# A hybrid decoder step: two weight slices scaled by their largest values, the first cast on GpSimd, loaded ahead of the second token tile, and the bias-table matmuls at later places in the program

## The chip, the cores and the metric

One core of a Trainium2 chip runs the whole program. Its engines are TensorE (matmuls, PE in the profile, with weight loads listed as PEld), VectorE (DVE), ScalarE (ACT), GpSimd (POOL) and SyncE (SP), whose queue issues nearly all transfers. The metric is the device time of one execution in microseconds (us), the median of several runs.

## The reference

One layer and one inference step, for a prompt of 2048 rows of 1024 and 8 sample rows:

```
h = rmsnorm(x, norm_g)
z = h @ w_in          # one matrix, its columns split among three mixers and their gates
A: q 512 | k 128 | v 128 | gate 512      sliding window of 128, 8 heads, 2 kv heads,
                                         logits = q.k/8 + rel_bias, learned sink per head
B: u 512 | v 512 | gate 512              chunked gMLP: u * (W_s v + b), causal 128x128
C: q 256 | k 256 | v 512 | gate 512 | r 16   gated linear attention, chunks of 64
x = x + concat[A*silu(gA), B*silu(gB), C*silu(gC)] @ w_out
y = rmsnorm(x, final gain)
```

The bias of mixer A depends on the distance between query and key alone, so the program makes one table of it (128 x 8 x 256) and adds it to the scores of every token tile.

## The kernel before, in words

**Numbers.** Values in fp32 are held as two fp16 parts, a high one (a cast of the scaled value) and a low one (the remainder, scaled value minus high part). Each product is three matmul passes, high by high, high by low, low by high, accumulated in one PSUM bank.

**Tokens.** There are 16 tiles of 128 tokens, two to a chunk of 256. `h_tile` (called through `norm_split`) squares a loaded tile on ScalarE with a row sum (L244), works out the reciprocal root of the mean on VectorE in a chain of 128x1 instructions (L246, then L124 to L134), casts the high part on ScalarE (L248), makes the low part on VectorE (L249), and has each part transposed by a DMA on SP (L258), which fills `hT`, the left or right side of every projection matmul. Loads of tiles are issued on SP by `x_load` (L240).

**Weight slices.** `prep_slice` brings a group of columns of `w_in` onto the chip in four parts (L164). Here matter A1 (k, v and r: 272 columns), A0 (q: 512) and A2 (gate: 512). `sq` squares each quarter with a row sum on ScalarE (L179), `sq2` adds over partitions with a matmul by ones (L185), bounds the scale and rounds it to a power of two (L187 to L192), and `split` makes, for each of 8 blocks, the high part on ScalarE (L203) and the low part on VectorE (L204). The A1 and A0 stages live in buffers named `hb`, A1's result in `s`, A0's in `sl`; `gs` is the scale by row, `invs` its inverse.

**Units.** Matmuls come in units: `unit_va` (v and r of one tile, through `mm_tok`, L307), `unit_k` and `unit_q` (k, and a quarter of q, of one chunk, through `mm_col`, L296), `unit_gate` (L307, then tanh on ScalarE L486 and a product on VectorE L487). Each writes a bank `pp` of which there are four; scores, tables and small sums use four banks `mx`.

**Bias table.** `lc_bias` multiplies the bias values by a table of distances (L384), copies the result, writes it to DRAM (`e_d`) and reads it back so that each partition holds a shifted row (`Lp`). `lc_bm` mirrors that with four fp32 matmuls of 128x512 (L398), and VectorE scales each into `BM`, which the scores' eviction (L510) reads.

**Order.** The function is written as a straight program. Side work is put in by `at(t, f)`, where t is a count of matmul columns issued so far divided by 2400, and `tick` runs what is due:

```
at(1.0, lambda: h_tile(2))
at(2.0, lc_bias)
at(7.0, lc_bm(0))
at(9.0, lc_bm(1))
```

A scheduler then reorders the instructions into one queue for each engine, and each engine works through its own in order. An instruction wrapped in `tc.keep_in_program_order` keeps its place among its engine's instructions. Scores of tile n are due at 17 + 6.5 x (2n), tanh and evictions follow their matmuls. Before the first unit come, in this order: load of tile 0, small constants, load of tile 1, loads of A1, first part of A0, `h_tile(0)`, A1's `sq` and `sq2`, `h_tile(1)`, A1's two halves of `split`, and the rest.

Of the kernel before, what the change touches and what calls it, by code (L numbers as in the profile page):

```python
# [15 lines left out]
AF = mybir.ActivationFunctionType  # L16
ALU = mybir.AluOpType
AX = mybir.AxisListType
# [15 lines left out]
OFF = {}  # L34
# [9 lines left out]
def hybrid_step_kernel(ctx: ExitStack, tc: tile.TileContext, I, O):  # L44
    nc = tc.nc
    V, S, G, PE, SP = nc.vector, nc.scalar, nc.gpsimd, nc.tensor, nc.sync
# [20 lines left out]
    def nm(s):  # L67
        cnt[0] += 1
        return f"{s}_{cnt[0]}"

    def small(shape, dt=F32, tag=None):
        w = 1
        for d in shape[1:]:
            w *= d
        return sm.tile(shape, dt, tag=tag or f"sm{w}", name=nm("sm"), bufs=1 if tag in ONE else 2 if tag in TWO else 8 if w <= 16 else 4)
# [4 lines left out]
    def mbank():  # L80
        return psm.tile([128, 512], F32, tag="mx", name=nm("mx"))

    def hbuf(shape, dt):
        return hp_.tile(shape, dt, tag="hT", name=nm("hb"))

    def slot(shape, dt):
        return sl_.tile(shape, dt, tag="slot", name=nm("sl"))
# [30 lines left out]
    def chain(p, n):  # L118
        t = sm.tile([p, 8 * n], F32, tag=f"ch{n}", name=nm("ch"), bufs=CHB[n])
        return [t[:, i * n:(i + 1) * n] for i in range(8)]  # L120
# [16 lines left out]
    def pow2_scale(ch, base_inv, s_out, inv_out):  # L137
        T, e = ch[0].bitcast(I32), ch[1].bitcast(I32)
        V.tensor_scalar(out=e, in0=T, scalar1=24, scalar2=None, op0=ALU.logical_shift_right)
        si, ii = ch[2].bitcast(I32), ch[3].bitcast(I32)  # L140
        V.tensor_scalar(out=si, in0=e, scalar1=-1.0, scalar2=205.0, op0=ALU.mult, op1=ALU.add)
        V.tensor_scalar(out=ii, in0=e, scalar1=1.0, scalar2=float(base_inv), op0=ALU.mult, op1=ALU.add)
        V.tensor_scalar(out=s_out.bitcast(I32), in0=si, scalar1=23, scalar2=None, op0=ALU.logical_shift_left)
        V.tensor_scalar(out=inv_out.bitcast(I32), in0=ii, scalar1=23, scalar2=None, op0=ALU.logical_shift_left)  # L144
# [2 lines left out]
    LOADP = {}  # L147
    INVI = {}

    def prep_slice(name, idx, cols, stage, dst, nload=1):  # L150
        n = sum(w for _, w in cols)
        inv = invs[:, idx:idx + 1]
        INVI[name] = inv
        st = {}

        def load_part(a, b):
            if "sg" not in st:
                st["sg"] = stage()
            for ap, k0, k1 in st["sg"]:
                lo, hi = max(a, k0), min(b, k1)  # L160
                c = 0
                for off, w in cols:
                    if lo < hi:
                        SP.dma_start(out=ap[:, lo - k0:hi - k0, c:c + w],  # L164
                                     in_=w_in[lo * 128:hi * 128, off:off + w].rearrange("(k p) n -> p k n", p=128))
                    c += w

        def load():
            for a in range(0, 8, 2):
                load_part(a, a + 2)  # L170

        def sq():
            st["dst"] = dst()
            SL[name] = st["dst"]
            acc = small([128, 4])
            for ap, k0, k1 in st["sg"]:
                for k in range(k0, k1, 2):
                    jk = st["dst"][:, 0, k:k + 2, :].bitcast(BF16)
                    S.activation(out=jk, in_=ap[:, k - k0:k - k0 + 2], func=AF.Square, accum_out=acc[:, k // 2:k // 2 + 1])  # L179
            st["acc"] = acc  # L180

        def sq2():
            acc = st["acc"]
            ps = mbank()
            PE.matmul(ps[:, 0:4], ones, acc, start=True, stop=True)  # L185
            ch = chain(128, 1)
            V.tensor_reduce(out=ch[5], in_=ps[:, 0:4], axis=AX.X, op=ALU.add)  # L187
            V.tensor_scalar(out=ch[0], in0=ch[5], scalar1=gmax2, scalar2=2e-20, op0=ALU.mult, op1=ALU.max)
            s = ch[4]
            pow2_scale(ch, 39, s, inv)  # L190
            gs = sm.tile([128, 8], F32, tag="gs", name=nm("gs"), bufs=3)
            V.tensor_scalar(out=gs, in0=gcol, scalar1=s, scalar2=None, op0=ALU.mult)  # L192
            st["gs"] = gs

        def split(a, b):
            def f():
                for ap, k0, k1 in st["sg"]:
                    for k in range(max(a, k0), min(b, k1)):
                        src = ap[:, k - k0, :]
                        hi = st["dst"][:, 0, k, :]  # L200
                        lo = st["dst"][:, 1, k, :]
                        gk = st["gs"][:, k:k + 1]
                        S.activation(out=hi, in_=src, func=AF.Copy, scale=gk)  # L203
                        V.scalar_tensor_tensor(out=lo, in0=src, scalar=gk, in1=hi, op0=ALU.mult, op1=ALU.subtract)  # L204
            return f

        LOADP[name] = [(lambda a=a: load_part(a, a + 2)) for a in range(0, 8, 2)]
        return [load, sq, sq2, split(0, 4), split(4, 8)]

    def stage_h(n):  # L210
        def f():
            return [(hbuf([128, 4, n], F32), 0, 4), (hbuf([128, 4, n], F32), 4, 8)]
        return f
# [6 lines left out]
    def dst_slot(n):  # L220
        return lambda: slot([128, 2, 8, n], F16)

    def dst_one(n):
        return lambda: one.tile([128, 2, 8, n], F16, tag="s1", name=nm("s1"))
# [7 lines left out]
    def x_bufs(j):  # L232
        if not xst:
            xst[0], xst[1] = slot([128, 4096], F32), slot([128, 4096], F32)
        b = xst[j // 2][:, (j % 2) * 2048:(j % 2 + 1) * 2048]
        return b[:, 0:DM], b[:, DM:2 * DM].bitcast(F16).rearrange("p (a b) -> p a b", a=2)

    def x_load(t):
        xt, _ = x_bufs(t % 4)
        SP.dma_start(out=xt, in_=xp[t * 128:(t + 1) * 128, :])  # L240
# [10 lines left out]
    def h_tile(t):  # L251
        c, j = divmod(t, 2)
        if j == 0:
            h_alloc(c)
        xt, xh = x_bufs(t % 4)
        norm_split(xt, xh, 128)
        for hl in range(2):
            SP.dma_start_transpose(out=hT[c][:, hl, :, j * 128:(j + 1) * 128], in_=xh[:, hl, :])  # L258
# [17 lines left out]
    def at(t, *fs):  # L276
        for f in fs:
            cnt[0] += 1
            bisect.insort(EV, (t, cnt[0], f))
# [71 lines left out]
    def startup_consts():  # L351
        G.memset(ones, 1.0)
        make_identity(nc, ident)
        SP.dma_start(out=gcol, in_=I["norm_g"][0].rearrange("(k p) -> p k", p=128))
        gm = small([128, 1])
        V.tensor_reduce(out=gm, in_=gcol, axis=AX.X, op=ALU.max, apply_absolute_value=True)
        ps = mbank()
        PE.matmul(ps[:1, 0:128], gm, ident, start=True, stop=True)
        m1 = small([1, 1])
        V.tensor_reduce(out=m1, in_=ps[:1, 0:128], axis=AX.X, op=ALU.max)  # L360
        ps2 = mbank()
        PE.matmul(ps2[:, 0:1], ones[0:1, :], m1, start=True, stop=True)
        g1 = small([128, 1])
        V.tensor_copy(out=g1, in_=ps2[:, 0:1])
        V.scalar_tensor_tensor(out=gmax2, in0=g1, scalar=2.0, in1=g1, op0=ALU.mult, op1=ALU.mult)

    lc = {}
# [26 lines left out]
    def lc_bm(half):  # L394
        def f():
            for q in range(2):
                ps = mbank()
                PE.matmul(ps, lc["fl"], lc[half][:, 2 * q:2 * q + 2, :].rearrange("p a b -> p (a b)"),  # L398
                          start=True, stop=True)
                V.tensor_scalar(out=BM["t"][:, half * 4 + 2 * q:half * 4 + 2 * q + 2, :].rearrange("p a b -> p (a b)"),  # L400
                                in0=ps, scalar1=rS, scalar2=-3e38, op0=ALU.mult, op1=ALU.max)
        return f
# [894 lines left out]
        return out  # L1297

    if True:
        prA1 = prep_slice("A1", 0, [(OFF["ka"], 256), (OFF["lr"], 16)], stage_h(272), dst_one(272))  # L1300
        prA0 = prep_slice("A0", 1, [(OFF["qa"], 512)], stage_h(512), dst_slot(512))
        prA2 = prep_slice("A2", 2, [(OFF["ga"], 512)], stage_h(512), dst_slot(512))
        x_load(0)
        startup_consts()
        x_load(1)
        prA1[0]()
        LOADP["A0"][0]()
        h_tile(0)
        prA1[1]()
        prA1[2]()  # L1310
        h_tile(1)
        prA1[3]()
        prA1[4]()
        LOADP["A0"][1]()
        for f in LOADP["A0"][2:]:
            f()
# [39 lines left out]
        at(1.0, lambda: h_tile(2))  # L1356
        at(2.0, lc_bias)
        at(3.0, lambda: h_tile(3))
        at(7.0, lc_bm(0))
        at(9.0, lc_bm(1))  # L1360
        for t in range(4, NTILE):
            at(HT0 + HTD * (t - 4) - HTL, lambda t=t: x_load(t))
            at(HT0 + HTD * (t - 4), lambda t=t: h_tile(t))
# [161 lines left out]
```

## Time and profile before

| what | value |
|---|---|
| median of 3 runs | 1195.62 us (1194.37 to 1195.87) |
| the profiled execution | 1196.05 us, of which the span of the trace is 1194.3 us |
| mean granted TensorE clock | 0.988 |
| TensorE matmuls | 1137.6 us busy (95%), 7637 instructions |
| TensorE weight loads | 662.2 us (55%), beside the matmuls |
| VectorE | 674.9 us (57%), 2229 |
| ScalarE | 481.5 us (40%), 967 |
| GpSimd | 72.5 us (6%), 49 |
| DMA | 128.63 MB, mean 108 GB/s |

Busy time is an average over very different stretches of the program. The profile lists instructions by line of the program, with the time at which one began, how long it took, and, in square brackets, how long its engine stood idle before it and which event ended that. Names of buffers are given without their numbers.

### The profile page before, as it was taken

The page shows a single profiled execution, that of the slowest core. Times are in us where ns is not written, and L with a number is a line of the kernel's source. Part 1 is how long each engine was busy: PE and PEld are TensorE (multiplying, and loading weights), DVE is VectorE, ACT ScalarE, POOL GpSimd, SP SyncE. Part 2 cuts the span into 40 slices and gives each one's busy share as a digit, 9 for nine tenths or more (in the row PEclk, how much of TensorE's full clock was granted, in tenths as well). Part 3 has the DMA queues.
Part 4 walks back from the last instruction along what each step waited for, and adds up shares of the span by engine and source line. Part 5 has one row for each costly group of instructions (what it writes and reads, how often), then busy time and mean ns, then how long its engine had stood idle before and what let it go on. Part 6 is the DMA issues. An engine that isn't in the chain of part 4 may idle for free.

```text
span 1194.3 us, 19596 instructions
## 1 busy us (share of the span) xinstructions
PE 1137.6 (95%) x7637; PEld 662.2 (55%) x7637; DVE 674.9 (57%) x2229; ACT 481.5 (40%) x967; POOL 72.5 (6%) x49
## 2 busy tenths in 40 slices
PE   4997899989999999999999999999999999999997
PEld 3756577776554544444465567566665543444443
DVE  5787866658685355576284355645545643544442
ACT  7776765567671021552265411412212131322220
POOL 0012222222120000000000000000000000000000
PEclk9998999999999999999999999999999999999999
DMA  9679964444454002000054521220114446766641
GB/s 268 165 125 198 192 152 89 73 80 123 90 144 112 18 22 83 10 18 18 18 186 117 210 55 31 95 89 18 54 44 128 122 123 159 206 160 165 167 124 54
DMA packets 196912, 128.63 MB, mean 108 GB/s; under 512 B 155921, under 2 KB 170394, under 8 KB 196818
## 3 DMA queue, kind: packets, MB, share of 16 engines
q1 hardware_dynamic: 196818, 127.36, 41.5%
q8 instruction: 60, 0.98, 0.4%
q14 instruction: 34, 0.28, 0.1%
HBM read 66.36 MB, written 23.63 MB: 75 GB/s over the span
## 4 chain that ended last, share of the span: by engine, by line
PE 59%; DVE 4%; DMA 3%; ACT 2%; issue 1%; SPq 1%; DVEq 0%; ACTq 0%
PE pp L307 31%; PE pp L1008 14%; PE pp L296 6%; DMA hb<-sl 1%; PE mx L867 1%; PE mx L671 1%; PE mx L849 1%; PE mx L873 1%; PE mx L881 1%; PE mx L320 1%; DMA sl<-y_d 1%; ACT sl L977 1%; SPq L989 1%; DVE sl L997 1%; DMA sl<-in_w_in_dram 0%
## 5 line engine op out<-in xcount | busy, mean ns | idle before, releaser
L307 PE MATMUL pp<-sl,hb 128*128 128x512 f16 x2304 | 518.7, 381 | 1.3 <-DVE qk L477 1.3
L307 PEld LDWEIGHTS <-hb 128*128 128x128 f16 x2688 | 248.9, 99 | 271.6 <-issue 15.5
L1008 PE MATMUL pp<-hb,hb 128*128 128x512 f16 x1152 | 251.2, 379 | 2.5 <-DMA hb<-sl 2.4
L1008 PEld LDWEIGHTS <-hb 128*128 128x128 f16 x1152 | 111.6, 98 | 140.3 <-DMA hb<-sl 5.3
L296 PE MATMUL pp<-hb,sl 128*128 128x256 f16 x1536 | 178.6, 274 | 8.9 <-DVE yy L487 8.8
L296 PEld LDWEIGHTS <-sl 128*128 128x128 f16 x1536 | 149.4, 99 | 31.8 <-issue 11.7
L549 POOL TENSOR_TENSOR phb<-Lp,pha 128x1024 f16<-128x1024 f32 (+1 forms) x32 | 66.4, 2075 | 285.4 <-ACT pha L548 268.2
L1011 DVE SCALAR_TENSOR_TENSOR sl<-pp,finv,sl 128x512 f32<-128x512 f32 x32 | 23.9, 747 | 85.5 <-PE pp L1008 85.5
L486 ACT ACTIVATE yy<-pp,scal 128x512 f32<-128x512 f32 x48 | 32.6, 680 | 84.7 <-PE pp L307 68.7
L994 ACT ACTIVATE sl<-sl 128x1024 f32<-128x1024 f32 (+1 forms) x16 | 16.9, 1055 | 116.6 <-DVE sl L1011 114.5
L538 ACT ACTIVATE Lp<-Lp,sm 128x256 f32<-128x256 f32 (+1 forms) x128 | 62.3, 488 | 0.1
L510 DVE CUSTOM_DVE_ANT_0 Lp<-mx,BM,scal 128x256 f32<-128x256 f32 (+1 forms) x128 | 55.0, 471 | 1.3 <-PE mx L506 0.5
L487 DVE SCALAR_TENSOR_TENSOR yy<-yy,pp 128x512 f32<-128x512 f32 x48 | 32.7, 681 | 38.5 <-ACT yy L486 38.5
L623 ACT ACTIVATE kk<-pp,invs 128x512 f32<-128x512 f32 x16 | 10.9, 683 | 95.5 <-PE pp L307 95.5
L477 DVE SCALAR_TENSOR_TENSOR qk<-pp,qk 64x256 f16<-64x256 f32 x64 | 26.9, 422 | 35.5 <-ACT qk L476 34.7
L978 DVE SCALAR_TENSOR_TENSOR sl<-sl,ch 128x1536 f16<-128x1536 f32 (+1 forms) x17 | 30.9, 1816 | 20.4 <-ACT sl L977 20.3
L977 ACT ACTIVATE sl<-sl,ch 128x1536 f16<-128x1536 f32 (+1 forms) x17 | 26.8, 1575 | 32.1 <-DVE ch L144 32.1
L637 DVE BATCH_NORM_STATS2 sm<-kk 128x6 f32<-128x512 f32 x16 | 11.0, 690 | 50.3 <-ACT kk L623 50.3
L506 PE MATMUL mx<-kk,qk 128*128 128x256 f16 (+1 forms) x256 | 33.9, 274 | 4.8 <-DVE sm L510 4.8
L307 PE MATMUL pp<-s,hb 128*128 128x144 f16 x384 | 30.2, 237 | 5.9 <-DMA hb<-sl 3.6
L204 DVE SCALAR_TENSOR_TENSOR sl<-sl,gs,sl 128x512 f16<-128x512 f32 x48 | 32.7, 745 | 3.3 <-ACT sl L203 3.2
L548 ACT CAST pha<-Lp 128x1024 f16<-128x1024 f32 (+1 forms) x32 | 32.4, 1012 | 2.4 <-DMA pt<-pha 1.9
(320 smaller groups left out, 1234.6 us busy)
## 6 DMA issues: line engine op xcount, KB each, us to landing
sl<-in_x_prompt_dram SPq DMA_DIRECT2D x32, 512.0 KB
sl<-in_w_in_dram SPq DMA_DIRECT2D x24, 512.0 KB
sl<-in_w_out_dram SPq DMA_DIRECT2D x6, 2048.0 KB
sl<-y_d SPq DMA_DIRECT2D x16, 768.0 KB
y_d<-yy SPq DMA_DIRECT2D x32, 256.0 KB
out_dram<-sl SPq DMA_DIRECT2D x15, 512.0 KB
hb<-in_w_in_dram SPq DMA_DIRECT2D x8, 512.0 KB
y_d<-Lp SPq DMA_DIRECT2D x8, 512.0 KB
```

What stands on the lines that cost most here:

```text
L204: V.scalar_tensor_tensor(out=lo, in0=src, scalar=gk, in1=hi, op0=ALU.mult, op1=ALU.subtract)
L296: PE.matmul(ps[:m, :CT], w[:, wl, k, c0:c0 + m], h[:, hl, k, :], start=(n == 0), stop=(n == 23))
L307: PE.matmul(ps[:, :n_], h[:, hl, k, j * 128:(j + 1) * 128], w[:, wl, k, c0:c0 + n_], start=(n == 0), stop=(n == 23))
L486: S.activation(out=g, in_=ps, func=AF.Tanh, scale=hg)
L487: V.scalar_tensor_tensor(out=g, in0=g, scalar=1.0, in1=ps, op0=ALU.add, op1=ALU.mult)
L506: PE.matmul(pv[:, hh, :], Qt[c][:, h // 2, h % 2, j * 128:(j + 1) * 128], Kt[c][:, 2 * hb + hl, ko:ko + W], start=(hl == 0), stop=(hl == 1))
L510: V.tensor_tensor_reduce(out=L[:, i, :], in0=pv[:, hh, :], in1=BM["t"][:, 4 * hb + i, 256 - W:256], scale=cS, scalar=-3e38, op0=ALU.add, o ...
L538: S.activation(out=L[:, i, :], in_=L[:, i, :], func=AF.Exp, bias=nb[:, i:i + 1], accum_out=den[:, i:i + 1])
L548: S.copy(P[0], L)
L549: G.tensor_tensor(out=P[1], in0=L, in1=P[0], op=ALU.subtract)
L977: S.activation(out=d["h"][:, 0, :], in_=d["y"], func=AF.Copy, scale=s)
L1008: PE.matmul(ps, d["yT"][:, hl, k, :], wo[k // 2][:, wl, k % 2, cs], start=(n == 0), stop=(n == 35))
```

## The change

Five things are different. A1 and A0 are scaled by a bound from the largest absolute value of each quarter's rows (a reduce on VectorE, squared afterwards) and no longer from the sum of squares on ScalarE. A1's eight high parts are cast on GpSimd. The load of the second token tile is issued after A1's four loads and no longer before them. `h_tile(1)` is written after both halves of A1's `split`. The four table matmuls come at 12 and 14, not 7 and 9, and keep their place in the program.

```
-    def prep_slice(name, idx, cols, stage, dst, nload=1):
+    def prep_slice(name, idx, cols, stage, dst, early=False):
...
             acc = small([128, 4])
+            if early:
+                for ap, k0, k1 in st["sg"]:
+                    for k in range(k0, k1, 2):
+                        V.tensor_reduce(out=acc[:, k // 2:k // 2 + 1], in_=ap[:, k - k0:k - k0 + 2], axis=AX.XY,
+                                        op=ALU.max, apply_absolute_value=True)
+                V.tensor_tensor(out=acc, in0=acc, in1=acc, op=ALU.mult)
+                st["acc"] = acc
+                return
...
-                        S.activation(out=hi, in_=src, func=AF.Copy, scale=gk)
+                        if name == "A1":
+                            G.tensor_scalar(out=hi, in0=src, scalar1=gk, scalar2=None, op0=ALU.mult)
+                        else:
+                            S.activation(out=hi, in_=src, func=AF.Copy, scale=gk)
                         V.scalar_tensor_tensor(out=lo, in0=src, scalar=gk, in1=hi, op0=ALU.mult, op1=ALU.subtract)
...
-                PE.matmul(ps, lc["fl"], lc[half][:, 2 * q:2 * q + 2, :].rearrange("p a b -> p (a b)"),
-                          start=True, stop=True)
+                tc.keep_in_program_order(PE.matmul(ps, lc["fl"], lc[half][:, 2 * q:2 * q + 2, :].rearrange("p a b -> p (a b)"),
+                                                   start=True, stop=True))
...
-        prA1 = prep_slice("A1", 0, [(OFF["ka"], 256), (OFF["lr"], 16)], stage_h(272), dst_one(272))
-        prA0 = prep_slice("A0", 1, [(OFF["qa"], 512)], stage_h(512), dst_slot(512))
+        prA1 = prep_slice("A1", 0, [(OFF["ka"], 256), (OFF["lr"], 16)], stage_h(272), dst_one(272), early=True)
+        prA0 = prep_slice("A0", 1, [(OFF["qa"], 512)], stage_h(512), dst_slot(512), early=True)
...
         startup_consts()
+        prA1[0]()
         x_load(1)
-        prA1[0]()
         LOADP["A0"][0]()
         h_tile(0)
         prA1[1]()
         prA1[2]()
-        h_tile(1)
         prA1[3]()
         prA1[4]()
+        h_tile(1)
...
-        at(7.0, lc_bm(0))
-        at(9.0, lc_bm(1))
+        at(12.0, lc_bm(0))
+        at(14.0, lc_bm(1))
```

Lines are added, so from the square in `sq` up to the cast in `split` a line carries a number greater by 8, and behind it by 11: the low part of a slice is L215, that of a tile L260, the transposes L269, tile loads L251, the token-stationary matmul L318, the query matmul L307, the table matmul L409.

**VectorE, where the second tile's scale is worked out.** Before: `ch_174` is tile 1's chain, `gs_172` and `s_14` belong to A1, and the last row is the tile's low part.

```order
L126 TENSOR_SCALAR ch_174<-ch_174 128x1
L204 SCALAR_TENSOR_TENSOR s_14_156<-hb_126,gs_172,s_14_156 128x272
L130 SCALAR_TENSOR_TENSOR ch_174<-ch_174 128x1
...
L134 SCALAR_TENSOR_TENSOR ch_174<-ch_174 128x1
L204 SCALAR_TENSOR_TENSOR s_14_156<-hb_127,gs_172,s_14_156 128x272 x2
L249 SCALAR_TENSOR_TENSOR sl_105<-sl_105,ch_174 128x1024
```

After: `ch_191` is tile 1's chain, `hb_136` and `hb_137` are A0's stage, `sm_229` its maxima, `hb_125` and `hb_126` A1's stage.

```order
L126 TENSOR_SCALAR ch_191<-ch_191 128x1
L179 TENSOR_REDUCE sm_229<-hb_136 128x1
L215 SCALAR_TENSOR_TENSOR s_14_156<-hb_125,gs_173,s_14_156 128x272 x4
L215 SCALAR_TENSOR_TENSOR s_14_156<-hb_126,gs_173,s_14_156 128x272 x4
L130 SCALAR_TENSOR_TENSOR ch_191<-ch_191 128x1
L179 TENSOR_REDUCE sm_229<-hb_136 128x1
L134 SCALAR_TENSOR_TENSOR ch_191<-ch_191 128x1
L179 TENSOR_REDUCE sm_229<-hb_137 128x1
```

All eight low parts of A1 and all four reduces of A0 now stand ahead of the last steps of that chain.

**TensorE, the bias table.** Before: `pp_555` is the third tile's v unit, and the scores of tile 0 (`kk`, `qk`) follow the table.

```order
L307 MATMUL pp_555<-s_14_156,hb_282 128x144
L398 MATMUL mx_415<-Lp_328,sm_225 128x512
L398 MATMUL mx_418<-Lp_328,sm_225 128x512
L398 MATMUL mx_448<-Lp_330,sm_225 128x512
L398 MATMUL mx_451<-Lp_330,sm_225 128x512
L185 MATMUL mx_515<-sm_478,ones 128x4
L307 LDWEIGHTS hb_282
```

After: `pp_460` and `pp_501` are the first chunk's third and fourth query units.

```order
L307 MATMUL pp_460<-hb_139,sl_228 128x256
L409 MATMUL mx_482<-Lp_330,sm_226 128x512
L409 MATMUL mx_485<-Lp_330,sm_226 128x512
L307 LDWEIGHTS sl_228
...
L307 MATMUL pp_501<-hb_139,sl_228 128x256
L409 MATMUL mx_511<-Lp_332,sm_226 128x512
L409 MATMUL mx_514<-Lp_332,sm_226 128x512
L193 MATMUL mx_517<-sm_468,ones 128x4
```

The table's matmuls stand in two pairs earlier in the row of TensorE, each inside a query unit.

**SP, loads of token tiles near the attention of tile 1.** Before: `sl_106` and `sl_105` are the buffers of the tiles, `pt` and `yy` belong to the attention.

```order
L240 DMA sl_106<-in_x_prompt_dram 128x1024
L563 DMA_TRANSPOSE pt_1074<-pha_1065 128x8x128
L563 DMA_TRANSPOSE pt_1074<-phb_1066 128x8x128
L588 DMA y_d<-yy_1002 128x512
L240 DMA sl_106<-in_x_prompt_dram 128x1024
L240 DMA sl_105<-in_x_prompt_dram 128x1024
L258 DMA_TRANSPOSE hb_1585<-sl_105 128x8x128 x2
```

After:

```order
L269 DMA_TRANSPOSE hb_1587<-sl_105 128x8x128 x2
L251 DMA sl_106<-in_x_prompt_dram 128x1024
L251 DMA sl_105<-in_x_prompt_dram 128x1024
L574 DMA_TRANSPOSE pt_1076<-pha_1067 128x8x128
L574 DMA_TRANSPOSE pt_1076<-phb_1068 128x8x128
L599 DMA y_d<-yy_1004 128x512
```

Both loads moved ahead of the attention's two transposes and its store.

## The prediction, made before the changed kernel was run

> **What bounds the kernel now.** I read the stretches first, then TensorE's waits, then the order of time around the longest of them.
>
> ```profile
> 0.00:50.00 50.00, 30.12 (x209) 22.66 (x210) 30.67 (x104) 34.07 (x67) 1.51 (x10) 0.97 0.93 257
> 50.00:200.00 150.00, 135.01 (x1280) 100.56 (x1279) 116.16 (x483) 102.36 (x266) 30.47 (x16) 0.97 0.72 146
> 200.00:640.00 440.00, 428.94 (x2903) 243.11 (x2902) 266.29 (x843) 203.81 (x428) 38.25 (x21) 0.99 0.28 69
> 640.00:1194.00 554.00, 543.48 (x3251) 295.91 (x3249) 261.82 (x802) 141.28 (x208) 2.30 (x2) 0.99 0.40 114
> ```
>
> After the stretch, its length and commas come PE, PEld, DVE, ACT and POOL busy, then clock, DMA share, GB/s. TensorE is idle 19.9 us in the first 50, 15.0 in the next 150, and 21.6 in the 994 after. So the kernel is bound by matmuls, except at its start and while the 16 token tiles are still being normalised beside the first attention tiles. The edit touches just those two stretches.
>
> ```profile
> 22.98 0.42 PE L307 MATMUL pp<-s,hb 128*128 128x144 f16 x2 [3.62 <-DMA hb<-sl]
> ...
> 24.14 2.85 PE L307 MATMUL pp<-s,hb 128*128 128x144 f16 x22
> ...
> 29.82 4.97 PE L296 MATMUL pp<-hb,sl 128*128 128x256 f16 x44
> 34.72 0.81 PE L384 MATMUL mx<-yy,relx 33*8 33x384 f32 x2
> ...
> 45.35 5.16 PE L398 MATMUL mx<-Lp,sm 128*128 128x512 f32 x8 [2.61 <-DMA Lp<-e_d]
> ...
> 50.55 0.61 PE L506 MATMUL mx<-kk,qk 128*128 128x128 f16 x8
> ...
> 108.07 0.80 PE L296 MATMUL pp<-hb,sl 128*128 128x256 f16 x3 [6.23 <-DVE yy L487]
> ...
> 136.76 0.74 PE L506 MATMUL mx<-kk,qk 128*128 128x256 f16 x4 [2.91 <-DVE sm L510]
> ```
>
> ```profile
> PE pp L296 <- DVE yy L487: 8.8, 3, 6.2
> ...
> PE mx L506 <- DVE sm L510: 4.8, 4, 2.9
> ...
> PE pp L307 <- DVE qk L477: 1.3, 1, 1.3
> ```
>
> At 24.14 TensorE gets the second token tile's transposes and then runs without a break to 42.74, where it waits 2.61 for the bias table's data. The table's eight passes end at 50.35. Later it waits 14.9 us for VectorE (8.8 + 4.8 + 1.3), nearly all between 50 and 200. A long wait also costs clock:
>
> ```profile
> 47.22 0.34 PEld L398 LDWEIGHTS mx<-Lp,sm 128*128 128x128 f32 x1 [0.52 <-issue]
> 48.08 0.32 PEld L398 LDWEIGHTS mx<-Lp,sm 128*128 128x128 f32 x1 [0.52 <-issue]
> ...
> 49.07 0.19 PEld L398 LDWEIGHTS mx<-Lp,sm 128*128 128x128 f32 x1 [0.24 <-issue]
> 49.49 0.19 PEld L398 LDWEIGHTS mx<-Lp,sm 128*128 128x128 f32 x1 [0.24 <-issue]
> ```
>
> ```profile
> 100.00:120.00 20.00, 13.77 (x139) 11.69 (x139) 14.90 (x76) 14.32 (x33) 4.25 (x2) 0.83 0.88 190
> ```
>
> Passes of the table stand 0.86 apart right after the wait and 0.42 later. In 100:120 a mean clock of 0.83 means 20 x 0.17 x 2 = 6.8 us at half speed. Some 5 us of it came after work resumed, costing about 2.6. The wait at 136.76 I charge 1.6 likewise.
>
> **The change, part by part: the second tile comes late.** Rows of the start:
>
> ```profile
> 6.16 0.15 DVE L246 TENSOR_SCALAR ch<-ch 128x1 f32<-128x1 f32 x1 [0.64 <-ACT sl L244]
> ...
> 7.94 0.16 DVE L134 SCALAR_TENSOR_TENSOR ch<-ch 128x1 f32<-128x1 f32 x1
> ...
> 8.65 0.66 ACT L179 ACTIVATE s<-hb 128x544 bf16<-128x544 f32 x1 [2.52 <-DMA hb<-in_w_in_dram]
> ...
> 14.36 3.41 ACT L203 ACTIVATE s<-hb,gs 128x272 f16<-128x272 f32 x8 [0.97 <-DVE ch L246]
> ...
> 14.92 0.50 DVE L204 SCALAR_TENSOR_TENSOR s<-hb,gs,s 128x272 f16<-128x272 f32 x1 [0.16 <-ACT s L203]
> ...
> 18.17 1.15 ACT L248 ACTIVATE sl<-sl,ch 128x1024 f16<-128x1024 f32 x1 [0.40 <-DVE ch L134]
> ...
> 19.36 1.29 DVE L249 SCALAR_TENSOR_TENSOR sl<-sl,ch 128x1024 f16<-128x1024 f32 x1 [0.45 <-ACT sl L248]
> ...
> 24.15 0.16 DVE L187 TENSOR_REDUCE ch<-mx 128x1 f32<-128x4 f32 x1 [0.19 <-PE mx L185]
> ...
> 26.06 0.22 DVE L130 SCALAR_TENSOR_TENSOR ch<-ch 128x1 f32<-128x1 f32 x1
> ```
>
> ```profile
> L904 DVE TENSOR_REDUCE ch<-yy 128x4 f32<-128x512 f32 x16 | 10.9, 682 | 20.7 <-ACT yy L902 20.7
> ```
>
> Eight squares leave ScalarE, eight maxima come onto VectorE. No row has this reduce; the nearest takes 0.68 for 512 columns, so 544 columns cost about 0.72 and 1024 between 1.15 and 1.36; I take 1.25. That is 7.9 us more on VectorE. The load order itself is worth little: the first A1 part landed by 8.65, and without the second tile's 512 KB ahead I estimate 6.6 (bounds 5.5 and 8.6). But it is VectorE, in order, that uses it. The first tile's scale took 6.16 to 8.10; now three reduces of A1 and a small one stand inside it, so it ends near 6.6 + 1.9 + 3 x 0.72 + 0.6 = 11.3. The ScalarE cast (1.1) follows, then the tile's low half (1.3), which stands ahead of A1's scale. The scale (1.1 more) is ready near 15.5, not 14.3.
>
> Now the eight A1 casts on GpSimd. No row has this either: its two-input subtract of 512 columns and a copy of 128 bound it, and by columns between them it is 0.62.
>
> ```profile
> L549 POOL TENSOR_TENSOR phb<-Lp,pha 128x512 f16<-128x512 f32 x2 | 2.3, 1158 | 66.8 <-ACT pha L548 66.8
> ...
> L270 POOL COPY hs<-h 128x128 f16<-128x128 f16 x1 | 0.3, 291 | 2.1 <-DMA h<-hs_d 2.1
> ```
>
> ```profile
> 90.58 2.13 POOL L549 TENSOR_TENSOR phb<-Lp,pha 128x1024 f16<-128x1024 f32 x1 [8.51 <-ACT pha L548]
> ...
> 91.42 1.31 DVE L551 TENSOR_TENSOR sm<-sm,sm 128x4 f32<-128x4 f32 x1
> ```
>
> ```profile
> L551 DVE TENSOR_TENSOR sm<-sm,sm x32: 150/161/2047, 65.3 to 355.5; 128x4 f32<-128x4 f32 x32
> ```
>
> These show a collision: a four-column VectorE operation with two SBUF inputs takes 0.16, but 1.31 when GpSimd is busy, ending where GpSimd ends. A1's remainders (0.50, spaced 0.52) have two SBUF inputs too. So casts and remainders take turns: 1.25 for A0's first reduce, which stands ahead of them and covers two casts, then 8 x 0.52 = 4.2, plus six uncovered casts, 3.7. If they do not collide, the 3.7 falls away. Behind them in VectorE's queue stand A0's other three reduces (3.75), with the second tile's last scale steps and small rows between (1.7). Its scale is therefore ready at 15.6 + 1.25 + 4.2 + 3.7 + 3.75 + 1.7 = 30.2, or 26.5 without collision; the cast that waits for it started at 18.17. Its low half stands behind A0's scale as well (24.15 to 26.28 before, plus 0.4) and starts near 33.1 or 29.4, not 19.36. TensorE gets it 13.7 or 10 later. I take **+13**, since the collision is in the trace. Meanwhile ScalarE is idle and hides nothing.
>
> The Trainium skill (GPSIMD Engine Reference, section Key points) says that GpSimd shares its SBUF interfaces with VectorE and contends with VectorE instructions that have two SBUF inputs. The trace agrees for a two-input GpSimd operation; no row shows a cast, and by that rule the term is 13, without it 10.
>
> **The bias table.** TensorE's order keeps four table matmuls, but earlier in its row than before: inside the third and fourth query units. Before: 42.74 to 50.35 is 7.6 us, for eight passes that need 8 x 0.43 = 3.4 at full clock. Between the matmul at L384 and the table's data lay 45.35 - 34.72 = 10.6; now 71 matmuls of 0.11 lie between, 7.8, so the wait would be 2.8. The transfer no longer stands behind a token load, so I take 1.4 (0 to 2.8). Gain 7.6 - 3.4 - 1.4 = **-2.8** (-4.2 to -1.4). Queued behind such a wait are 57 projection matmuls and the first scores, so a longer one would cost one for one. At 50.55, then, the new kernel is 10.2 late.
>
> **What is given back between 50 and 200.** Two of the long waits come from loads of token tiles standing late in SyncE's queue:
>
> ```profile
> 98.83 1.81 SPq L240 DMA_DIRECT2D sl<-in_x_prompt_dram  x2
> ...
> 104.24 1.06 ACT L244 ACTIVATE sl<-sl 128x1024 bf16<-128x1024 f32 x1 [2.73 <-DMA sl<-in_x_prompt_dram]
> ...
> 128.41 1.06 ACT L244 ACTIVATE sl<-sl 128x1024 bf16<-128x1024 f32 x1 [4.52 <-DMA sl<-in_x_prompt_dram]
> ```
>
> ScalarE stops at these squares, and the gate's tanh and the query casts queue behind them; VectorE and TensorE wait in turn. In the new order the loads issued at 98.83 stand ahead of two attention transposes and a store that came before them, and the last tile's load comes earlier too. Of 6.23 + 2.6 I expect 3.5 + 1 to stay, since VectorE has 7.9 more to do: -4.3. Of 2.91 + 1.6, 1.3 stays: -3.2. Of the other waits, 14.9 - 6.2 - 2.9 = 5.8, I expect 1.5 back. Together **-9.0**; the bounds are 0 (the backlog moves along with everything) and -15 (both waits and their clock go, and some of the rest).
>
> The sum: +13 - 2.8 - 9.0 = +1.2 against 1196.05, the profiled execution's time, which stands 0.43 above the median of the runs: 1196.8 on that scale. A measurement can tell 0.2%, or 2.4 us, from no change.
>
> **Rivals.** *Slower:* the give-back fails. VectorE is the backlogged engine from 50 to 110, and 7.9 us of new work there keeps the tanh's drain as late as before. Of -9 only -2 to -5 remains: +5 to +8, 1201 to 1204. For it: 116 of 150 us busy, and TensorE waits for VectorE by name. Against it: at the worst moment VectorE itself waits for ScalarE's squares. It decides once less than 7.8 is given back. *Faster:* casts and remainders overlap (10, not 13), and the earlier loads remove both long waits, -13: 10 - 2.8 - 13 = -5.8, 1189.8. For it: both waits end on a token load. Against it: the collision row. *Not what it says:* the reduces hide behind the weights' landing and the second tile is only about 3 late; then +3 - 2.8 with 3 given back, about -3, 1192.8. Against it: every A0 reduce stands ahead of that tile's last scale step, whatever lands when.
>
> **How the numbers follow.** The forecast, a late start nearly repaid and within 0.2%, 0.37; slower rival 0.34; the two faster ones together 0.29. The range leaves out about one in ten on each side: 1190 to 1203.5. The forecast's own range is 1193.4 to 1198.
>
> **What would show it.** Right: TensorE's first long run begins near 37, not 24; VectorE's remainders at L215 stretch from 16.8 to about 24.7; the table matmuls wait under 3 us and run at 0.43; the scores of tile 0 start near 60; the wait ahead of the third chunk's first query unit (6.23 before) is under 4. Wrong: if the second tile's cast starts before 22, the first term has failed; if 50 to 200 keeps 15 us of idle TensorE, the give-back has.

## The result, and the profile after

The changed kernel takes 1206.12 us (median of five runs, 1204.71 to 1207.93) against 1195.62 before: 1.0098 times as long, 95% interval 1.0083 to 1.0113, or 10 to 13.5 us. It is slower, and above the range. Its profiled execution took 1207.93, with a span of 1206.1 (before 1194.3), so the traces differ by 11.8. Runs of one kernel spread by 2 to 13 us here, and two profiled executions below (e2 and e13) lie 3 to 5 under the median of their kernel; so the sums are made in the traces, and the ratios say what is certain.

The stretches of the changed kernel:

```profile
0.00:50.00 50.00, 21.75 (x146) 16.44 (x147) 35.65 (x107) 23.10 (x39) 9.04 (x18) 1.00 0.86 223
50.00:200.00 150.00, 134.45 (x1226) 98.65 (x1225) 115.27 (x460) 96.88 (x245) 28.52 (x15) 0.94 0.74 149
200.00:640.00 440.00, 429.29 (x2967) 247.70 (x2966) 268.05 (x856) 199.72 (x431) 40.39 (x22) 0.99 0.29 72
```

TensorE is 8.4 us less busy in the first 50, and between 50 and 200 it stands idle for 15.5 us, where the forecast had most of the 15.0 vanish. It also got through 54 matmuls fewer there, at a lower clock (0.94, 0.97 before). After 200 nothing more is lost. VectorE's busy time from 50 to 200 is 115.3 (116.2 before): the new reduces are all done by then.

TensorE in order of time (start, duration, what it is; in brackets the idle time before it and what ended that):

```profile
34.26 2.82 PE L318 MATMUL pp<-s,hb 128*128 128x144 f16 x22 [1.94 <-DMA hb<-sl]
...
49.51 1.98 PE L409 MATMUL mx<-Lp,sm 128*128 128x512 f32 x4 [1.33 <-DMA Lp<-e_d]
...
53.30 1.88 PE L409 MATMUL mx<-Lp,sm 128*128 128x512 f32 x4
...
58.29 0.61 PE L517 MATMUL mx<-kk,qk 128*128 128x128 f16 x8
...
99.69 0.60 PE L517 MATMUL mx<-kk,qk 128*128 128x256 f16 x4 [2.41 <-DVE sm L521]
...
113.78 0.49 PE L307 MATMUL pp<-hb,sl 128*128 128x256 f16 x3 [2.72 <-DVE yy L498]
...
124.95 1.01 PE L517 MATMUL mx<-kk,qk 128*128 128x256 f16 x4 [2.51 <-DVE sm L521]
...
145.18 0.60 PE L517 MATMUL mx<-kk,qk 128*128 128x256 f16 x4 [1.70 <-DVE sm L521]
...
154.71 0.60 PE L517 MATMUL mx<-kk,qk 128*128 128x256 f16 x4 [1.17 <-DVE sm L521]
...
159.99 0.80 PE L307 MATMUL pp<-hb,sl 128*128 128x256 f16 x3 [3.71 <-DVE yy L498]
```

The second tile is there at 34.26, 10.1 late. The table waits 1.33 and runs at full clock, its passes 0.43 apart. Tile 0's scores start 7.7 late. The wait ahead of the third chunk's first query unit (113.78) fell from 6.23 to 2.72, a little more than forecast, and TensorE is 5.7 late there (108.07 before). But a wait of 2.41 now stands ahead of it, where the same matmul waited 0.30 before. Of the waits behind it, counted by the same matmuls, 2.51 and 1.17 are new, 3.71 was 1.38, and only 1.70 was longer before (2.91). At 160 TensorE is 10.5 late again.

The new wait of 2.41 is of the old kind. ScalarE stood still for the load of a token tile, and the tanh that VectorE needed ahead of the scores' eviction was queued behind that square (tanh at 97.44, VectorE's product at 98.14, the first eviction at 98.74):

```profile
94.32 1.06 ACT L255 ACTIVATE sl<-sl 128x1024 bf16<-128x1024 f32 x1 [4.15 <-DMA sl<-in_x_prompt_dram]
```

VectorE at the start, and the casts and remainders as a group (minimum, median and maximum of one, in ns):

```profile
14.28 1.21 DVE L179 TENSOR_REDUCE sm<-hb 128x1 f32<-128x1024 f32 x1
15.41 0.72 DVE L215 SCALAR_TENSOR_TENSOR s<-hb,gs,s 128x272 f16<-128x272 f32 x1
16.35 0.72 DVE L215 SCALAR_TENSOR_TENSOR s<-hb,gs,s 128x272 f16<-128x272 f32 x1 [0.22 <-POOL s L212]
...
21.98 0.50 DVE L215 SCALAR_TENSOR_TENSOR s<-hb,gs,s 128x272 f16<-128x272 f32 x1 [0.22 <-POOL s L212]
...
22.53 1.21 DVE L179 TENSOR_REDUCE sm<-hb 128x1 f32<-128x1024 f32 x1
...
29.81 1.28 DVE L260 SCALAR_TENSOR_TENSOR sl<-sl,ch 128x1024 f16<-128x1024 f32 x1
```

```profile
L212 POOL TENSOR_SCALAR s<-hb,gs x8: 961/962/966, 14.4 to 21.0; 128x272 f16<-128x272 f32 x8
L215 DVE SCALAR_TENSOR_TENSOR s<-hb,gs,s x8: 503/720/722, 15.4 to 22.0; 128x272 f16<-128x272 f32 x8
```

A remainder leaves every 0.94 us, at the pace of GpSimd's cast, and takes 0.72 while the next cast runs beside it; the last, with no cast beside it, takes 0.50. The second tile's low part starts at 29.81 (19.36 before).

### The profile page after: what moved, and what is told of

It is laid out like the page before. It is cut to its first block, busy times and chain, and to the rows that moved or that the text cites. A ratio compares the mean times of both kernels' runs of the same rounds, so it can differ in the third digit from the quotient of the medians.

```text
span 1206.1 us, 19595 instructions
## 1 busy us (share of the span) xinstructions
PE 1140.1 (95%) x7637; PEld 663.7 (55%) x7637; DVE 687.3 (57%) x2239; ACT 472.2 (39%) x943; POOL 80.3 (7%) x57
## 4 chain that ended last, share of the span: by engine, by line
PE 56%; DVE 4%; DMA 4%; ACT 3%; issue 1%; SPq 1%; DVEq 0%; ACTq 0%
PE pp L318 30%; PE pp L1019 13%; PE pp L307 6%; DMA hb<-sl 2%; PE mx L878 1%; PE mx L682 1%; PE mx L860 1%; PE mx L884 1%; ACT sl L988 1%; PE mx L892 1%; DMA sl<-in_w_out_dram 1%; PE mx L331 1%; DMA sl<-y_d 1%; SPq L1000 1%; DVE sl L1008 1%
## 5 line engine op out<-in xcount | busy, mean ns | idle before, releaser
L318 PE MATMUL pp<-sl,hb 128*128 128x512 f16 x2304 | 518.3, 381 | 0.0
L318 PEld LDWEIGHTS <-hb 128*128 128x128 f16 x2688 | 248.6, 99 | 277.2 <-issue 15.6
L307 PE MATMUL pp<-hb,sl 128*128 128x256 f16 x1536 | 181.6, 277 | 7.5 <-DVE yy L498 6.9
L307 PEld LDWEIGHTS <-sl 128*128 128x128 f16 x1536 | 150.8, 99 | 32.0 <-issue 9.7
L318 PE MATMUL pp<-s,hb 128*128 128x144 f16 x384 | 29.8, 238 | 13.1 <-DMA hb<-sl 7.9
L215 DVE SCALAR_TENSOR_TENSOR sl<-sl,gs,sl 128x512 f16<-128x512 f32 x48 | 32.7, 744 | 3.0 <-ACT sl L214 2.9
```

The costliest lines, as they stand in the source:

```text
L307: PE.matmul(ps[:m, :CT], w[:, wl, k, c0:c0 + m], h[:, hl, k, :], start=(n == 0), stop=(n == 23))
L318: PE.matmul(ps[:, :n_], h[:, hl, k, j * 128:(j + 1) * 128], w[:, wl, k, c0:c0 + n_], start=(n == 0), stop=(n == 23))
```

## The experiments

From tile 0's scores on, TensorE's row (the order of its instructions) is the same in nearly all these kernels up to far behind the stretch in question, so the start of its n-th matmul (counted from zero) can be compared between kernels. This is worked out from the traces: how late the 60th is (the second tile has arrived), the 500th and the 1316th, against the kernel before, and how long the stretch between those two took.

```
kernel                                60th   500th  1316th   500th to 1316th
before                                 0       0       0         95.9
e2  A1 by maxima, A0 by squares       +4.8    +5.6    +4.7       95.0
e3  both by squares                   +4.1    +6.0    +5.4       95.3
e5  before, casts on GpSimd           +2.9    +1.7    +0.8       95.0
changed                               +9.7    +6.8   +11.7      100.8
e1  changed, casts on ScalarE         +5.7    +2.9    +6.9       99.9
e10 changed, A1 by squares            +8.8    +7.7   +13.0      101.1
e9  before, load moved                -2.0    -0.9    +3.2      100.0
e4  changed, tile order back          +4.4    +2.9   +10.8      103.8
e6  changed, transposes in order      +9.4    +6.9    +1.1       90.1
e8  before, transposes in order       +0.1    -1.6    -7.0       90.5
```

In the first group the rows of all engines from tile 0's scores on are those of before; in the second (changed, e1, e10) those of the changed kernel. e9 and e4 have a third order, which from 82 us on is the same in both, but not between 51 and 82. In e1, e2, e3, e4 and e10 the rest of the change is as it was.

**e1, casts on ScalarE in the changed kernel.** Nothing else moves in any row.

```
-    if name == "A1": G.tensor_scalar(out=hi, in0=src, scalar1=gk, ...)
+    S.activation(out=hi, in_=src, func=AF.Copy, scale=gk)
```

> The changed kernel, but A1's eight high parts are cast on ScalarE again; the order on every other engine is that of the changed kernel. In the changed kernel the eight remainders on VectorE stand 0.94 us apart, each released by GpSimd. Theory 'passed through' (a late second tile moves everything behind it by as much): remainders 0.52 apart, so the second tile is about 2.9 earlier (7.1 us for eight become 4.2), its projections begin near 31.4 instead of 34.3, and the kernel takes 1206.1 - 2.9 = 1203.2. Rival 'middle order' (the time is lost between 60 and 165 us, by a new order of transfers on SyncE, and the start has slack): 1205.5 to 1206.5, unchanged.

1203.66, ratio 1.0077 (1.0058 to 1.0096). Remainders took 0.50 each, 15.1 to 18.0, and the second tile came 4.0 earlier (60th matmul: +5.7, not +9.7). The traces end 4.8 apart and the ratios 2.5. The ratio, 1204.8 on the forecast's scale, lies between the two theories, and its interval overlaps that of the changed kernel; it is the traces that show no slack at the start.

**e2, A0 by squares; e3, both by squares; e4, the second tile's work written ahead of A1's casts again; e5, GpSimd's casts alone in the kernel before.**

```
e2: -  prA0 = prep_slice("A0", ..., early=True)      +  prA0 = prep_slice("A0", ...)
e3: the same for prA1 and prA0
e4: +  h_tile(1)  ahead of prA1[3](), and not behind prA1[4]()
e5: in the kernel before, for "A1": +  G.tensor_scalar(out=hi, in0=src, scalar1=gk, ...)
```

> The changed kernel, but A0 is scaled by its sum of squares on ScalarE again, so only A1 keeps the maxima. VectorE's row then has no A0 reduce ahead of the second tile's scale, its low part stands ahead of A0's scale, the table's matmuls fall back to where they were before, and the transfers between 60 and 165 us stand in the row of SyncE as before the change. Theory 'passed through': the low part starts near 24.5 (29.8 in the changed kernel, 19.4 before), the second tile is 4 to 5 late against before, and the kernel takes 1195.6 + 4.5 = 1200. Rival 'middle order': with the old order in the middle the late start is absorbed, 1195.5 to 1197. Rival 'A1's part is what costs': 1204 to 1206.

> The changed kernel with sums of squares on ScalarE for both slices; GpSimd's casts, the load order, the place of the second tile's work and of the table's matmuls as changed. Remainders still follow GpSimd at 0.94 apart and stand ahead of all of the second tile's last scale steps. Theory 'passed through': the low part of the second tile starts near 24 (19.4 before) and the kernel takes about 1195.6 + 4.5 = 1200. Rival 'middle order': SyncE's row between 60 and 165 us is as before the change, so 1195.5 to 1197.

> The changed kernel, but the second tile's work is written ahead of A1's casts again, as before the change. VectorE's row then has two of A0's four reduces behind the second tile's scale and its low part ahead of A0's scale; the remainders still follow GpSimd. Theory 'passed through': scale ready near 15.4 + 8 x 0.94 = 23, one reduce (1.2) ahead of the low part, which starts near 24.5; 4.5 to 5 late, and the kernel takes about 1200. Rival 'middle order': SyncE's row in the middle is nearly that of before, so 1195.5 to 1197.5. Rival 'reduces on VectorE cost their 7.9 us wherever they stand': 1203 to 1205.

> The kernel before, with one edit: A1's eight high parts are cast on GpSimd. From the third token tile on, the order on all engines is exactly that of before. Theory 'passed through': a cast of 128x272 on GpSimd takes 0.94 (as in the changed kernel), where ScalarE's took 0.43, so the eighth remainder is 8 x 0.5 = 4 later; ScalarE, freed, has the second tile's cast earlier, but its low part stands behind the eighth remainder on VectorE, so the second tile is about 3 late and the kernel takes 1195.6 + 3 = 1198.6, with the two long waits (6.2 and 2.9) unchanged. Rival 'absorbed': the two long waits shrink by what is lost at the start, 1195 to 1196.5.

e2: 1203.37, ratio 1.0071 (1.0055 to 1.0088); e3: 1199.55, 1.0041 (1.0027 to 1.0056); e4: 1205.42, 1.0087 (1.0072 to 1.0103); e5: 1199.05, 1.0033 (1.0020 to 1.0046). "Absorbed" and "middle order absorbs" fell: all three kernels with the old order (e2, e3, e5) are slower than before, and both long waits are there as before. In the traces e2 and e3 kept their lateness in full to the 1316th matmul; e5 kept 0.8 of 2.9. TensorE in e2, from 108 to 143:

```profile
113.58 0.80 PE L307 MATMUL pp<-hb,sl 128*128 128x256 f16 x3 [5.98 <-DVE yy L498]
...
141.49 1.01 PE L517 MATMUL mx<-kk,qk 128*128 128x256 f16 x4 [3.09 <-DVE sm L521]
```

They began 107.60 and 138.40 us into the span and ended 5.5 and 4.7 later than in the kernel before: the loads behind them had moved along with everything (the two issued at 98.83 before went at 104.26). So a late start of 4 to 5 us is handed on whole. A0's maxima account for half of the late second tile (e2: +4.8 left of 9.7), GpSimd's casts for most of the rest (e5: +2.9; e1: -4.0); A1's maxima cost 0.7 to 0.9 there (e2 against e3, the changed kernel against e10). What they cost in the whole time is not settled: e2's ratio (1204.1 on the forecast's scale) lies in the range of its rival "A1's part is what costs" and 3.6 us above e3's, but the changed kernel took 3.1 less than e10, which lacks A1's maxima. e4's time is near that of its third rival, that the reduces cost 7.9 wherever they stand, but not for that reason: it was only 2.9 late at the 500th, yet it ended nearly as late as the changed kernel. Its stretch took 103.8. That was the first sign that the order in the middle has a price of its own.

**e9, the load moved alone, and e10, A0's maxima without A1's**, were made to test that.

```
e9: in the kernel before:  -  x_load(1); prA1[0]()     +  prA1[0](); x_load(1)
e10: in the changed kernel, prA1 without early=True
```

> The kernel before, with one edit of the change alone: the load of the second token tile is issued after A1's four loads. VectorE makes the second tile's low part at the same place of its row as before, so its start is at most 1 late. But the scheduler now interleaves token tiles and attention between 60 and 165 us in another way, close to that of the changed kernel with its tile order put back, which lost 8 us there. Theory 'order and start add up': 1195.5 + 6 to 8 = 1201 to 1203.5, with the lateness growing between 60 and 200 us. Rival 'only the start counts': 1195 to 1196.5.

> The changed kernel, but A1 is scaled by its sum of squares on ScalarE again; A0 keeps its maxima. From the third tile on, the rows of VectorE, ScalarE and SyncE are exactly those of the changed kernel; the start differs. A0's four reduces still stand ahead of the second tile's scale. Theory 'order and start add up': the second tile is 9 to 10 late, as in the changed kernel, and the middle adds its 4 to 5 again: 1204.5 to 1206.5. Rival 'A1's maxima are what costs': 1200 or less.

e9: 1199.89, ratio 1.0047 (1.0033 to 1.0060), at or a little under the low end of what was expected; e10: 1209.17, 1.0124 (1.0101 to 1.0147), over it. Both go with "add up": e9 was 0.9 ahead at the 500th matmul and 3.2 behind at the 1316th, e10 went from +7.7 to +13.0. The stretch between the two, one row for each kernel (start and end; its length; then, as in the stretches above, PE, PEld, DVE, ACT and POOL busy, clock, DMA share, GB/s). Before:

```profile
88.33:184.21 95.88, 82.25 (x817) 62.07 (x816) 68.94 (x282) 61.79 (x160) 21.76 (x11) 0.95 0.85 178
```

e3, with the order of before:

```profile
94.28:189.61 95.33, 82.40 (x817) 61.87 (x816) 69.14 (x282) 61.47 (x158) 21.88 (x11) 0.93 0.85 178
```

The changed kernel, and then e1, with its order:

```profile
95.17:195.94 100.77, 85.84 (x817) 63.92 (x816) 73.55 (x288) 62.46 (x165) 21.53 (x11) 0.92 0.80 162
```

```profile
91.23:191.09 99.86, 82.30 (x817) 60.87 (x816) 73.35 (x288) 62.82 (x165) 21.51 (x11) 0.97 0.80 164
```

The same 817 matmuls stand in each. Within each of the first two groups the length goes by the order, to 1.3 us, whatever the start. The pair e9 and e4 shows a limit of this: with the same rows from 82 us on, e4's stretch is 3.8 longer. Nearly all of that arises in its first 112 matmuls, where e4 waits 2.44 and 1.06 at 96 and 105 us and e9 does not (the changed kernel, e1 and e10 wait 2.4 to 2.7 at the same first place); behind them both take 90.1 to 90.2. So what the other engines still have before them at the 500th matmul counts too. And TensorE sets little of the length: in the changed kernel it is busy 3.5 us longer than in e1, at a lower clock, and idle 2.6 less (100.77 - 85.84 = 14.9 against 17.6), and the stretch is almost as long.

**e6, e7, e8, e12: other orders in the middle.** e6 and e8 keep the transposes of token tiles from the fifth on where the program has them, in the changed kernel and in the kernel before. e7 gives the softmax of the first eight tiles priority. e12 keeps the fifth to tenth tile's transposes only.

```
e6, e8, e12, in h_tile:
-    SP.dma_start_transpose(out=hT[c][:, hl, :, ...], in_=xh[:, hl, :])
+    i_ = SP.dma_start_transpose(out=hT[c][:, hl, :, ...], in_=xh[:, hl, :])
+    if t >= 4:   # e12: 4 <= t < 10
+        tc.keep_in_program_order(i_)
e7, around a_soft, a_exp and a_split of tiles 0 to 7:
+    with tc.high_priority(offset=300):
```

> The changed kernel, with one edit: transposes of token tiles from the fifth on keep their place in the program on SyncE, so that the attention's transposes are not queued behind them. TensorE's row is the same to the last matmul, and so is the start up to the scores of tile 0. Theory 'middle order' (some 5 us of the loss arise between 60 and 165 us because ScalarE's casts wait for transposes of the attention that stand behind loads and transposes of token tiles): that wait of ScalarE falls from 7.0 to 2 or less, and the kernel takes 1201 to 1203. Rival 'late start alone': 1205.5 to 1206.5. Rival 'token tiles become late': TensorE waits for transposed tiles, over 1208.

> The changed kernel, with one edit: the softmax of the first eight tiles is given priority over other side work, so it stands ahead of token tiles' work on VectorE, ScalarE and SyncE. TensorE's row and the start are those of the changed kernel. Theory 'middle order': the lateness at the scores of tile 0 stays near 7.7 and does not grow to 11.7 by 200 us; 1202 to 1204. Rival 'late start alone': 1205.5 to 1206.5. Rival 'token tiles become late': the loads wait longer for their buffers and the kernel takes over 1208.

> The kernel before, with the edit of the run on the changed kernel in which transposes of token tiles from the fifth on keep their place in the program. The start and TensorE's row are those of before; loads of tiles now stand ahead of the transposes that held them at 98.8 us. Theory 'middle order' (how token tiles and attention are interleaved on SyncE sets the two long waits, whatever the start): the wait of 6.2 at 108 us falls below 3 and the kernel takes 1190 to 1193. Rival 'the middle is set by the amount of work on VectorE and ScalarE': 1195 to 1196.5.

> The kernel before, with transposes of the fifth to tenth token tile kept in program order on SyncE and the later ones left to the scheduler. The run with all of them kept was 10 to 12 us ahead at 142 us and had lost it all again by 268 us, in new waits of 3.2, 1.8 and 2.5 and in clock. Theory 'the later waits come from the later transposes being kept': 1187 to 1191. Rival 'TensorE ahead of the attention must wait for it later': 1194 to 1196.

e6: 1202.79, ratio 1.0070 (1.0053 to 1.0087); e7: 1214.41, 1.0162 (1.0147 to 1.0178); e8: 1195.36, 1.0006 (0.9994 to 1.0018); e12: 1196.11, 1.0013 (0.9997 to 1.0030). What ScalarE's cast for the attention waits for, over 60 to 170 us (total, times, longest); before:

```profile
ACT pha L548 <- DMA pt<-pha: 1.7, 1, 1.7
```

changed:

```profile
ACT pha L559 <- DMA pt<-pha: 7.0, 3, 4.6
```

e6:

```profile
ACT pha L561 <- DMA pt<-pha: 0.2, 1, 0.2
```

e9:

```profile
ACT pha L548 <- DMA pt<-pha: 7.6, 2, 5.6
```

In the changed kernel's queue on SyncE the wait of 4.6 looks so:

```profile
106.62 6.24 SPq L269 DMA_TRANSPOSE hb<-sl  x4
112.91 1.05 SPq L251 DMA_DIRECT2D sl<-in_x_prompt_dram  x2
114.07 1.23 SPq L574 DMA_TRANSPOSE pt<-pha  x1
```

```profile
107.19 1.04 ACT L559 CAST pha<-Lp 128x1024 f16<-128x1024 f32 x1
...
119.76 1.04 ACT L559 CAST pha<-Lp 128x1024 f16<-128x1024 f32 x1 [4.57 <-DMA pt<-pha]
```

The attention's probabilities are cast by 108.2, but four transposes and two loads of token tiles stand ahead of their own transposes, the first of which goes at 114.07; the next cast waits until they are done. e6 removes this, and by the 900th matmul it was 3.7 ahead of the kernel before although its second tile came 9.4 late. So what the forecast had given back can be given back; the changed kernel's own order did not do it. e6's time is in the range of its theory and e8's in that of its rival, but neither tells the whole, for both lost their lead again: from the 1316th to the 2173rd matmul they took 91.2 and 90.8 us, where all of the first two groups took 84.3 to 84.6. e8 was 12 ahead at 142 us and level at 268. e12, which leaves the later transposes to the scheduler, was 12.3 ahead at the 900th matmul and 2.7 at the 1316th; its theory (1187 to 1191) fell too. e7, which held back the token tiles instead, only cost.

**e11, the second tile first.** The kernel before, A1 by maxima, casts on ScalarE, the table as in the change, `h_tile(1)` ahead of A1's scale.

> The kernel before with A1 scaled by its maxima on VectorE (A0 by squares), casts on ScalarE, the old order of loads, the second tile's work written ahead of A1's scale, the table as in the change. VectorE's row has the second tile's low part ahead of A1's eight remainders, so it starts near 15 instead of 19.4 and TensorE's wait of 3.6 at 22.98 goes; the middle order is neither that of before nor of the change. Theory 'order and start add up': start 3 to 4 early, the middle unknown, 0 to +8: 1192 to 1200. Rival 'only the start counts': 1191 to 1192.5.

1202.16, ratio 1.0060 (1.0038 to 1.0082), over both theories. The second tile's low part started at 17.36, 2 earlier and not 4, and A1's casts only at 17.24 (14.36 before): the first projections began 2.9 late, and the first query unit waited 3.2 at 33 us for A0's casts. At the 500th matmul the kernel was 2.6 late. Moving one start ahead put two others back.

**e13, e14, e15: loads of token tiles on GpSimd's queue (changed kernel, kernel before), and four tiles' transposes in order (kernel before).**

```
e13, e14, in x_load:  -  SP.dma_start(...)   +  (G if t >= 4 else SP).dma_start(...)
e15: as e12, with 4 <= t < 8
```

> The changed kernel, with one edit: loads of token tiles from the fifth on are issued from GpSimd's queue and no longer from SyncE's. TensorE's row is the same to the last matmul. Theory 'loads ahead of the attention's transposes cost the middle': ScalarE's wait for those transposes falls from 7.0 to 2 or less, the stretch from the 501st to the 1317th matmul, 100.8 us in the changed kernel and 95.9 before, falls to 97 or less, and the kernel takes 1202 or less. Rival 'the token tiles' own work': the stretch stays at 100 or more, 1205 to 1207. Rival 'GpSimd's queue holds the loads back behind its subtractions': ScalarE waits longer for loads and the kernel takes over 1208.

> The kernel before, with loads of token tiles from the fifth on issued from GpSimd's queue. Theory 'loads': ScalarE's waits of 8.7 for loads fall and with them TensorE's waits of 6.2 and 2.9, 1189 to 1192. Rival 'the token tiles' own work': 1195 to 1196.5. Rival 'GpSimd's queue holds the loads back': over 1198.

> The kernel before, with transposes of the fifth to eighth token tile kept in program order. Theory 'the lead can be kept if the later order is near that of before': 10 ahead at 142 us and at least 5 ahead at 270 us, 1189 to 1191. Rival 'TensorE ahead of the attention waits for it later whatever the order': the lead shrinks to 2 or less by 270 us, 1194 to 1196.5.

e13: 1215.33, ratio 1.0180 (1.0148 to 1.0211); e14: 1218.42, 1.0193 (1.0174 to 1.0212); e15: 1196.60, 1.0016 (1.0002 to 1.0029). Loads from GpSimd's queue made both kernels slower, already by the 500th matmul (e13 4.0 behind the changed kernel there, e14 12.5 behind the kernel before), and the stretch did not shrink (e13 101.9, e14 107.2). So they do not test the middle alone. e14 is 8.6 late at the 60th matmul: GpSimd issued loads of later tiles at 12.02 and 20.92, and the second tile's two transposes, which start at 19.32 as before (19.35), took SyncE 6.13 us and not 2.70; why is not shown. In e13 the wait for the attention's transposes fell only to 4.6; its time is that of its third theory, though ScalarE waited less for loads, not longer (1.4, in the changed kernel 6.2, over 60 to 170 us). e15 was only 2.5 ahead at the 900th matmul, so it did not have the lead that both its theories began from; ScalarE waited 8.5 for the attention's transposes and the stretch took 97.7; in e12 it waited 0.6 and the stretch took 95.2. So the wait for them goes with a long stretch in the changed kernel, e9 and e10 (7.2), and its absence with a short one in e6, but it does not measure the length by itself.

## Why the prediction was right and wrong, point by point

- **The second tile: +13 forecast, +10.1 measured** (34.26 against 24.14). The path was right: maxima, casts and remainders all stand ahead of its scale. Sizes: A1's scale, put at 15.5, was there by 14.3; its own terms (11.3, 1.1, 1.3 and 1.1) add up to 14.8. Behind the tile's scale the prediction's rows give 2.5, and it went on with 2.9; 2.9 was measured. A 128x1024 reduce took 1.21 (forecast 1.25). The collision was mis-sized and mis-shaped: casts and remainders run beside each other, the cast at 0.96 (0.62 forecast), the remainder stretched from 0.50 to 0.72. The spacing of 0.94 is thus GpSimd's own. The figure without taking turns, +10, is the one that came out, but by luck: of its terms A1's scale was 1.3 too late, the stretch of remainders 2.7 too short and the steps behind it 1.0 too long, which nearly cancel. By the rule of the Trainium skill (GPSIMD Engine Reference, section Key points) the two contend, and the trace agrees, with 0.22 per remainder (0.50 in e1, 0.72 here), which the cast's length hides.
- **The table: -2.8 forecast, -2.4 measured.** Before, 42.74 to 50.35 went to it; now 1.33 + 1.98 + 1.88 = 5.2. Wait 1.33 (forecast 1.4).
- **What is given back: -9.0 forecast, +4.0 measured.** This is the step that failed: 10.1 - 2.4 + 4.0 = 11.7, and with -9.0 in its place the measured start would have given -1.3. Up to the wait at 113.78 TensorE went from 7.7 late to 5.7, so 2.0 came back of the 4.3 forecast for that wait; behind it 6.0 were lost, where 4.7 more were to come back. The step rested on two things. First, that the loads behind the two long waits would keep their own time while TensorE came later. They did not: with the order unchanged (e2, e3, e5) both waits moved along, to within 0.3 us of their lengths. Second, that loads further forward in SyncE's queue only gain. The first wait did shrink, by 3.5 to 2.72 (forecast: 3.5 left), but a wait for another token load came ahead of it (2.41, for 0.30), and the loads now stand ahead of the attention's transposes, which the prediction noted and gave no price. Waits of 2.51, 1.70, 1.17 and 3.71 follow where 2.91 and 1.38 had been. The clock from 50 to 200, from which 2.6 and 1.6 were to come back in part, fell from 0.97 to 0.94. e9 shows that a new order can lose as much by itself: with a start 0.9 early it lost 4.1 us, though 3.8 of it behind the 972nd matmul, where the changed kernel lost 1.3.
- **The rivals.** The slower one (1201 to 1204) named the right sign and not the cause: VectorE's new work was done by 27 us, and from 50 to 200 it was as busy as before (115.3 against 116.2). The faster one was right about casts and remainders running together and wrong about the give-back; the third, a second tile only 3 late, did not come about.
- **The signs to look for** did their work: the first long run near 37 (34.26) and the remainders from 16.8 to 24.7 (15.4 to 22.5) came a little early; scores near 60 (58.29), the table's wait under 3, the wait ahead of the third chunk's query unit under 4 (2.72), and, for the give-back, 15 us of idle TensorE from 50 to 200 as the mark of failure (15.5).

Not settled: which rows of the new order carry its 4 to 5 us, and how much of it comes with what the other engines bring into the stretch (e4 against e9). Rows of VectorE, ScalarE and SyncE always changed together, and no run changed SyncE's alone. Nor is it shown why e6 and e8 lose their lead after 180 us.

## What to carry to other kernels

A wait that ends on a transfer is not a reserve: ask what issues the transfer, and if it is a queue that hangs on the delayed work, the wait can move along and give nothing back. When a small edit at the start lets a scheduler reorder a later stretch, price the two apart: compare the same matmuls by their count, in kernels that share the order and differ in the start, and the other way round. Where a stretch is as long with TensorE slow as with TensorE idle, its clock and its idle time are not costs to add up; some other chain sets most of the length.

## What the runs showed of the hardware that was not expected

- GpSimd's cast of 128x272 from fp32 to fp16 took 0.96 us in all eight places, twice ScalarE's 0.51 (e1), also beside a one-input reduce on VectorE.
- A VectorE operation with two SBUF inputs beside a one-input GpSimd cast is stretched by 0.22 (0.50 to 0.72), while beside GpSimd's two-input subtraction a four-column one took 1.31 before.
- With the loads of twelve token tiles issued from GpSimd's queue and not from SyncE's, and the order that came with it, the kernel before was 1.9% slower (e14); the changed kernel was 1.8% slower than the kernel before, where it had been 1.0% (e13).
